# A two-layer transformer block on one core: gates in four PSUM tiles, a step's pacing, and where two norms stand

## The chip, the cores and the metric

The kernel runs on one core of a Trainium2 chip. The time is what one execution takes on the device, in microseconds (us). The kernel before took 2803.42 us (median of three runs, 2800.37 to 2804.48).

Engine names in the profile: PE is TensorE (matrix products), DVE is VectorE, ACT is ScalarE, POOL is GpSimd, SP is SyncE, which here only issues DMAs. SBUF is the on-chip memory, PSUM the small accumulator memory that PE writes.

## The reference

Two layers work on 1024 tokens `x` and 256 context tokens `ctx` of width 1024. Cut to what matters:

```python
for l in range(2):
    mod = silu(c) @ w_ada[l] + b_ada[l]            # shift, scale, gate per column; the same with c_ctx
    h   = rms_norm(x, norm_g[l]) * (1 + scale) + shift          # and hc from ctx
    a_glu, a_gate, nq, nk, nv, n_gate, wq, wk, wv, w_gate, merge = split(h @ w_in[l])
    o_na = neighbourhood_attention(nq, nk, nv, ...)
    o_wa = window_attention(wq, wk, wv, ...)
    y_a = (silu(layer_norm(conv(glu(a_glu)))) * silu(a_gate)) @ w_proj_a
    y_b = (o_na * silu(n_gate)) @ w_proj_b
    y_c = (o_wa * silu(w_gate)) @ w_proj_c
    y = sigmoid(g_a) * y_a + sigmoid(g_b) * y_b + sigmoid(g_c) * y_c      # g_* from merge
    x = x + gate * (y @ w_o)
    # layer 0 does the same for ctx; layer 1 gives x alone
```

All is float32. The kernel returns x after layer 1.

## The kernel before

Everything is held transposed: features on the 128 partitions, tokens along the row. The tokens form three groups (`GROUPS`): 0 and 1 of 512 image tokens, 2 of the 256 context tokens. Layer 0 works on all three; the gates, projections and the output of layer 1 work on groups 0 and 1 only.

A float32 product is made of three: each operand is split into a high part and a low part (`hh`/`hl`, `ogh`/`ogl`, two planes of a weight), and PE does high by high, low by high and high by low for each of 8 chunks of 128 features (`product`, L714), 24 matmuls into one PSUM tile. The projections of the branches have 4 chunks, 12 matmuls.

**Order.** PE runs in the order of the program (`sched` asks for a manual schedule of PE). The other engines get an order from a list scheduler when the program is built; each engine then runs its instructions strictly in that order, and an instruction that waits holds all behind it. SP's DMA issues stand in such a queue too.

**PSUM.** `mm_tile` gives one of two tiles in turn (pool `ps_mm`, 2 buffers). `s_tile` gives the tiles of two further pools, `ps_s` and `ps_t`, in turn. `ps_tr` is one more tile, used for small products: the sums `ss_ps` and the broadcast `sr_ps` of a norm, and `ada_sum`. A new product into a tile waits until the last reader of the old one is done.

**A layer.** First the attention, with the projections of units (q, k, v columns) and GLU in between; then the gates of the merge; then branch b, c and a: for each branch the gate blocks and the projection. A gate block (`gate_blocks`, c = 0 to 3, one product per group) is `gate`: product into `gt_ps`, tanh on ACT, and an elementwise step on DVE (L852) that reads PSUM; then `gated`: GpSimd multiplies by the branch's values `ov` (L862), ACT rounds to the high part `ogh` (L863), and GpSimd subtracts for the low part `ogl` (L864). `project` then does 8 blocks f of products with `ogh`/`ogl`, in four PSUM tiles (`s_tile` and `mm_tile` in turn, `pp_ps`), and combines each with the merge gate `mg_in` that SP loads: L963 on DVE for branch b, L965 on DVE and L967 on GpSimd for c.

**Side work.** The modulation of the next layer (`ada_blocks`) is done on DVE beside these products: blocks of four steps, each a DMA of a piece of `w_ada` (`w_ada_s`, two buffers) and 4 instructions (L205, L207). In layer 1 only one of the two columns is needed, and a step has 2 instructions; there are 4 such blocks, 16 steps. Two small PE products (`ada_sum`, L183) sum a finished block up; they stand in PE's order three steps later. `Pace` spreads the steps: each PE chunk adds credit (its time times a share), and a step is issued while there is credit; each step yields its cost. Beside gate b a convolution's normalisation (`conv_norm`, L824, L831) is paced in the same way and finished before project b.

**From layer 0 to layer 1.** The output of layer 0 is normalised for layer 1. Group 0's norm is done within the output pass. Then unit 0 of layer 1 is projected: ten tiles of 128 tokens (0 to 3 of group 0, 4 to 7 of group 1, 8 and 9 of group 2), 8 chunks each, into the two `mm_tile` buffers; `out` evicts a tile: ACT L352, L358, L370 and DVE L353, L371. The norm of a group (`Norm.steps`) is: sums on PE (L252), a chain of small DVE steps (L257, L106 to L111), a diagonal on GpSimd (L261), a broadcast on PE (L264) copied by ACT (L265), and then for each of 8 chunks k DVE L272, ACT L273 (`hh`) and DVE L274 (`hl`). Groups 1 and 2 go through these steps after unit 0's first two tiles have been issued (L1264 to L1273).

Of the kernel before, what the change touches and what calls it, by code (L numbers as in the profile page):

```python
# [13 lines left out]
ALU = mybir.AluOpType  # L14
# [26 lines left out]
KC = 8  # L41
# [9 lines left out]
def hybrid_block_kernel(  # L51
# [9 lines left out]
    nc = tc.nc  # L61

    def f32(ap):
        return ap.bitcast(F32)
# [107 lines left out]
    def ada_blocks(items, pool):  # L172


        late = []

        def sums():
            while late:
                l, lc, j0, ncol, av = late.pop(0)
                pt = ps_tr.tile([128, 512], F32, tag="tr", name="ada_sum")  # L180
                for j in range(2):
                    for c in range(ncol):
                        nc.tensor.matmul(  # L183
                            pt[:, 2 * j + c:2 * j + c + 1], lhsT=av[:, c, j * 128:(j + 1) * 128], rhs=ones[:, 0:1],
                            start=True, stop=True
                        )
                nc.vector.tensor_tensor(
                    mods[l][:, j0:j0 + 2, 0:ncol], pt[:, 0:4].rearrange("p (j c) -> p j c", c=2)[:, :, 0:ncol],
                    lc["b_ada"][:, j0:j0 + 2, None].to_broadcast([128, 2, ncol]), ALU.add,
                )  # L190

        for l, lc, j0 in items:
            src = w_ada[l].rearrange("(k p) n -> p k n", p=128)
            ncol = 1 if l == L - 1 and j0 >= 16 else 2
            acc = pool.tile([128, 512], F32, tag="acc0", bufs=2, name="ada_acc")
            av = acc.rearrange("p (c n) -> p c n", c=2)
            for k0 in range(0, KC, 2):
                w = pool.tile([128, 512], F32, tag="acc1", bufs=2, name="w_ada_s")
                wv = w.rearrange("p (k n) -> p k n", k=2)
                nc.sync.dma_start(out=wv, in_=src[:, k0:k0 + 2, j0 * 128:j0 * 128 + 256])  # L200
                for k in range(k0, k0 + 2):
                    for c in range(ncol):
                        s = sc_t[:, k, c:c + 1]
                        if k == 0:
                            nc.vector.tensor_scalar(av[:, c], wv[:, 0], s, None, ALU.mult)  # L205
                        else:
                            nc.vector.scalar_tensor_tensor(  # L207
                                av[:, c], wv[:, k - k0], s, av[:, c], ALU.mult, ALU.add
                            )
                yield 2 * ncol * 490.0  # L210
                if k0 == 4:
                    sums()
            late.append((l, lc, j0, ncol, av))
        yield 6000.0
        sums()
# [168 lines left out]
    def project_unit(l, u, h, pa, st, ws=None, unit=None, begin=0):  # L384

        if ws is None:
            ws = unit_weights(wU[l, u], pa)
            yield SWITCH_NS
        unit = unit or Unit(l, u, pa, st)
        for t in range(begin, 10):  # L390
            ps = mm_tile("u_ps")
            for k in range(KC):
                ns = unit.chunk(t, k, ws[k], h, ps)
                if k < KC - 1:
                    yield ns
            unit.out(t, ps)
            yield ns
        unit.close()
# [277 lines left out]
    def run(gen):  # L676
        for _ in gen:
            pass
# [30 lines left out]
    def product(w, kn, hx, n, ps):  # L709

        hh, hl = hx
        for k in range(kn):
            for i, (b, a) in enumerate(((0, hh), (0, hl), (1, hh))):
                nc.tensor.matmul(  # L714
                    ps[:, 0:n], lhsT=w(k, b), rhs=a[:, k, 0:n],
                    start=(k == 0 and i == 0), stop=(k == kn - 1 and i == 2),
                )
            if k < kn - 1:
                yield 3 * max(n / 2.4, 107)
# [4 lines left out]
    def mm_tile(name):  # L724
        return ps_mm.tile([128, 512], F32, tag="mm", name=name)

    flip = [0]

    def s_tile(name):
        flip[0] ^= 1  # L730
        if flip[0]:
            return ps_s.tile([128, 1024], F32, tag="s", name=name)
        return ps_t.tile([128, 1024], F32, tag="t", name=name)
# [112 lines left out]
    def gate(w, h, gi, t):  # L846

        n = GROUPS[gi][1]
        ps = mm_tile("gt_ps")
        yield from product(w, KC, h[gi], n, ps)  # L850
        nc.scalar.activation(t, ps[:, 0:n], AF.Tanh, scale=0.5)
        nc.vector.scalar_tensor_tensor(t, t, 1.0, ps[:, 0:n], ALU.add, ALU.mult)  # L852
        yield 3 * max(n / 2.4, 107)

    def gated(br, c, gi, t, ov, og):

        o, n = GROUPS[gi]
        a0, a1 = t, ov[:, 0:n]
        if br == "b" and gi < 2:
            a0 = a0.rearrange("p (r b c) -> p r b c", r=8, b=8)  # L860
            a1 = a1.rearrange("p (b r c) -> p r b c", b=8, r=8)
        nc.gpsimd.tensor_tensor(a0, a0, a1, ALU.mult)  # L862
        nc.scalar.activation(og[gi][0][:, c, :], t, AF.Copy)  # L863
        nc.gpsimd.tensor_tensor(og[gi][1][:, c, :], t, f32(og[gi][0][:, c, :]), ALU.subtract)  # L864

    def gated_tiles(po, ngr):
        og = []
        for gi in range(ngr):
            n = GROUPS[gi][1]
            og.append((  # L870
                po.tile([128, 4, n], F32R, tag=f"ogh{gi}", name=f"ogh{gi}"),
                po.tile([128, 4, n], F32R, tag=f"ogl{gi}", name=f"ogl{gi}"),
            ))
        return og
# [55 lines left out]
    def gate_blocks(l, br, h, pw, px, og, ngr, side):  # L930

        ws = [load_block(wF[l, I0[br]], pw)]
        for c in range(4):
            w = ws.pop(0)
            if c < 3:
                ws.append(load_block(wF[l, I0[br] + c + 1], pw))
            for gi in range(ngr):
                o, n = GROUPS[gi]
                ov = px.tile([128, 544], F32, tag="cv", bufs=1, name="ov")
                nc.sync.dma_start(out=ov[:, 0:n], in_=act_d[br][c][:, o:o + n])  # L940
                t = pw.tile([128, 512], F32, tag="t", bufs=3, name="gt_t")[:, 0:n]
                along(gate(w, h, gi, t), side)
                gated(br, c, gi, t, ov, og)
# [110 lines left out]
    def advance(gen, tiles):  # L1054
        for _ in range(KC * tiles):
            next(gen)
# [19 lines left out]
    with side_pool(0, "st", False) as st:  # L1076
# [15 lines left out]
        step = norm.steps(0, xs[0], g)  # L1092
# [61 lines left out]
        unit0 = project_unit(0, 0, h, pa, state, ws0, units[0], 4)  # L1154
# [4 lines left out]
        step = norm.steps(0, xs[2], g)  # L1159
# [5 lines left out]
    for l in range(L):  # L1165
# [15 lines left out]
        for nm in ORDER:  # L1181
            i = int(nm[1])
# [23 lines left out]
        with side_pool(l, "pc", True) as pools["pc"]:  # L1206
# [6 lines left out]
            og = gated_tiles(po, ngr)  # L1213
# [6 lines left out]
        if l + 1 < L:  # L1220
            cols += [(l + 1, lc_next, j) for j in range(0, 16, 2)]
        side = Pace(ada_blocks(cols, px), SHARE[1])
        for br in "bca":
            if br != "b":
                og = gated_tiles(po, ngr)
# [31 lines left out]
        def first_norm():  # L1257
            yield
            yield from norms[0].steps(l + 1, y[0], g)

        step = first_norm()
# [3 lines left out]
        unit0 = project_unit(l + 1, 0, h, pa, state, ws0)  # L1265
        steps = [norms[gi].steps(l + 1, y[gi], g) for gi in (1, 2)]
        advance(unit0, 1)
        next(steps[0])
        next(steps[1])
        advance(unit0, 1)  # L1270
        for step in steps:
            run(step)
        run(unit0)  # L1273
        sw.close()
# [88 lines left out]
```

## Time and profile before

| | |
|---|---|
| median of three runs | 2803.42 us |
| the profiled execution: its own time / span in the trace | 2803.28 / 2801.5 us |
| PE busy | 2701.9 us (96%) |
| VectorE / ScalarE / GpSimd busy | 1775.5 (63%) / 1132.6 (40%) / 897.1 us (32%) |
| mean granted TensorE clock | 0.989 |

PE counts as busy from a matmul's start to its end, and matmuls overlap, so it is at 96% even where it isn't at its best rate; the gaps between matmuls and the stretches at a lower granted clock show where time is left. A wait list gives, for each engine, what an instruction waited for last. Granted clock 1.00 is the upper level (2.4 GHz), 0.5 the lower (1.2 GHz); a value between is a mean over the stretch.

### The profile page before, as it was taken

Reading aid. Unit: us, or ns where it says so; the run is one execution under the profiler, and the core shown is the slowest. Engines: PE = TensorE matmul, PEld = TensorE weight load, DVE = VectorE, ACT = ScalarE, POOL = GpSimd, SP = SyncE. Lnnn points to the kernel's source line nnn. Section 1 sums busy time; section 2 is a strip of 40 time slices with the busy share of each in tenths; the row PEclk is TensorE's granted clock in tenths of the full one; section 3 lists DMA queues with packets and bytes.
Section 4 is the critical chain, followed back from the end, with each engine's and each line's share of the span. In section 5 each row is a group of like instructions: output and inputs, shape, how many; then the busy total and the mean of one; then the engine's idle time right before and its main releaser. Section 6 shows DMA issues by size and latency. Waiting matters only on the chain. (4 is left out here: it accounts for less than half of the span.)

```text
span 2801.5 us, 43631 instructions
## 1 busy us (share of the span) xinstructions
PE 2701.9 (96%) x14996; PEld 2354.5 (84%) x14996; DVE 1775.5 (63%) x3816; ACT 1132.6 (40%) x2500; POOL 897.1 (32%) x1148
## 2 busy tenths in 40 slices
PE   7899999999999999999999899999999999989999
PEld 3899999988888887888888899989888788767887
DVE  4667776766699905777365566666665798351162
ACT  2466666666411114121333356655555322322220
POOL 0034465633300004256501133465434100426610
PEclk9999999999999999999999999999999999989999
DMA  7355443211233322745364355452212333263343
GB/s 249 102 167 151 132 126 99 72 55 39 88 113 122 121 87 89 215 131 151 113 201 131 99 152 155 134 141 76 74 54 69 114 131 121 82 195 106 102 146 110
DMA packets 321293, 337.35 MB, mean 120 GB/s; under 512 B 81840, under 2 KB 240688, under 8 KB 321072
## 3 DMA queue, kind: packets, MB, share of 16 engines
q1 hardware_dynamic: 300848, 296.81, 35.8%
q10 hardware_dynamic: 17280, 28.32, 2.7%
q0 software_dynamic: 2944, 9.44, 0.8%
q8 instruction: 118, 1.93, 0.3%
q14 instruction: 103, 0.84, 0.1%
HBM read 244.02 MB, written 90.44 MB: 119 GB/s over the span
## 5 line engine op out<-in xcount | busy, mean ns | idle before, releaser
L714 PE MATMUL mg_ps<-hh,wf 128*128 128x512 f32 (+1 forms) x1920 | 563.3, 373 | 2.3 <-POOL wf L670 1.3
L339 PE MATMUL u_ps<-wu,hh 128*128 128x384 f32 (+2 forms) x1872 | 487.2, 343 | 18.2 <-ACT hh L273 12.3
L714 PEld LDWEIGHTS mg_ps<-hh,wf 128*128 128x128 f32 x1920 | 347.2, 188 | 71.5 <-POOL wf L670 2.1
L670 POOL TENSOR_TENSOR wf<-rf,wf 128x512 fp32r<-128x512 f32 x114 | 152.5, 1338 | 674.9 <-ACT wf L669 674.7
L714 PE MATMUL mg_ps<-hl,wf 128*128 128x512 f32 (+1 forms) x960 | 358.6, 374 | 0.0
L608 POOL TENSOR_SCALAR p<-p,rd 128x640 f32<-128x640 f32 (+1 forms) x288 | 216.4, 752 | 407.4 <-DVE rd L606 235.8
L339 PEld LDWEIGHTS u_ps<-wu,hh 128*128 128x128 f32 x1872 | 320.8, 192 | 23.9 <-ACT hh L273 12.8
L600 ACT ACTIVATE p<-p,nmx 128x641 f32<-128x641 f32 (+3 forms) x288 | 222.1, 771 | 237.2 <-DVE nmx L596 113.6
L339 PE MATMUL u_ps<-wu,hl 128*128 128x384 f32 (+2 forms) x936 | 313.6, 335 | 0.7 <-DVE hl L274 0.7
L714 PE MATMUL gt_ps<-hh,wf 128*128 128x512 f32 (+1 forms) x960 | 287.5, 380 | 8.2 <-DVE gt_t L852 5.4
L669 ACT ACTIVATE wf<-rf 128x512 fp32r<-128x512 f32 x240 | 150.6, 628 | 354.7 <-PE pp_ps L714 184.9
L714 PE MATMUL pp_ps<-ogh,wf 128*128 128x512 f32 (+1 forms) x960 | 282.2, 377 | 3.0 <-ACT ogh L863 2.6
L618 DVE TENSOR_TENSOR pt<-tp,pt 128x640 fp32r<-128x640 f32 (+1 forms) x288 | 215.8, 749 | 100.3 <-ACT pt L617 97.9
L714 PEld LDWEIGHTS gt_ps<-hh,wf 128*128 128x128 f32 x960 | 176.5, 190 | 46.5 <-DVE gt_t L852 6.9
L914 ACT ACTIVATE mg_t<-mg_ps 128x512 f32<-128x512 f32 (+1 forms) x120 | 66.7, 555 | 365.0 <-PE mg_ps L714 350.6
L714 PEld LDWEIGHTS pp_ps<-ogh,wf 128*128 128x128 f32 x960 | 177.9, 192 | 37.5 <-ACT ogh L863 3.1
L714 PEld LDWEIGHTS mg_ps<-hl,wf 128*128 128x128 f32 x960 | 180.5, 188 | 31.3
L614 PE MATMUL tp<-ident,p 128*128 128x128 f32 x1280 | 187.5, 273 | 17.8 <-DVE pt L618 9.8
L772 DVE SCALAR_TENSOR_TENSOR cv_out<-cv_in,lc_conv_w,cv_out 128x1024 f32<-128x1024 f32 (+1 forms) x192 | 194.5, 1013 | 0.0
L614 PEld LDWEIGHTS tp<-ident,p 128*128 128x128 f32 x1280 | 153.6, 141 | 45.4 <-POOL p L608 13.4
L617 ACT ACTIVATE pt<-tp 128x640 fp32r<-128x640 f32 (+1 forms) x288 | 181.8, 631 | 20.9 <-PE tp L614 19.6
L714 PE MATMUL pp_ps<-ogl,wf 128*128 128x512 f32 (+1 forms) x480 | 181.5, 378 | 3.6 <-POOL ogl L864 3.6
(172 smaller groups left out, 5498.1 us busy)
## 6 DMA issues: line engine op xcount, KB each, us to landing
rf<-in_wF SPq DMA_DIRECT2D x144, 256.0 KB, 2.8
ru<-in_wU SPq DMA_DIRECT2D x104, 192.0 KB, 3.6
bias<-in_na_bias SPq DMA_DIRECT2D x96, 192.0 KB, 2.6
w_ada_s<-in_w_ada SPq DMA_DIRECT2D x64, 256.0 KB, 3.2
nrm<-qk_d SPq DMA_DIRECT2D x40, 320.0 KB, 4.0
rf<-in_wP SPq DMA_DIRECT2D x48, 256.0 KB, 2.7
rf<-in_wO SPq DMA_DIRECT2D x48, 256.0 KB, 3.2
v_d<-vr SPq DMA_DIRECT2D x80, 128.0 KB, 2.1
```

The costliest lines, as they stand in the source:

```text
L339: nc.tensor.matmul(ps[:, c0:UW], lhsT=a[:, k, off * 128:(off + 1) * 128], rhs=w[:, b, c0:UW], start=(k == 0 and i == 0), stop=(k == KC - 1 ...
L600: nc.scalar.activation(self.p[:, 0:n], self.p[:, 0:n], AF.Exp, bias=m, scale=1.0 if sink is None else -1.0, accum_out=self.den)
L608: nc.gpsimd.tensor_scalar(p, p, rd, 1.0, ALU.mult, ALU.mult)
L614: nc.tensor.transpose(tp[:, c * 128:(c + 1) * 128], self.p[:, c * 128:(c + 1) * 128], ident)
L617: nc.scalar.activation(self.pt[:, 0:nch, 0, :], tv, AF.Copy)
L618: nc.vector.tensor_tensor(self.pt[:, 0:nch, 1, :], tv, f32(self.pt[:, 0:nch, 0, :]), ALU.subtract)
L669: nc.scalar.activation(w[:, 0, 0:n, :], raw[:, 0:n, :], AF.Copy)
L670: eng.tensor_tensor(w[:, 1, 0:n, :], raw[:, 0:n, :], f32(w[:, 0, 0:n, :]), ALU.subtract)
L714: nc.tensor.matmul(ps[:, 0:n], lhsT=w(k, b), rhs=a[:, k, 0:n], start=(k == 0 and i == 0), stop=(k == kn - 1 and i == 2),)
L772: nc.vector.scalar_tensor_tensor(r, a[:, k:k + n], tap, r, ALU.mult, ALU.add)
L914: nc.scalar.activation(t[:, 0:n], ps[:, 0:n], AF.Tanh, scale=0.5)
```

## The change

Four edits. `gate` takes its PSUM tile from `s_tile` and `mm_tile` in turn, so four tiles instead of two. In `gated`, the low part of the last block of a branch (c = 3) is computed on VectorE instead of GpSimd: 15 instructions, 9 in layer 0 and 6 in layer 1. A modulation step always costs 4 x 490 ns in the pacing; before it was 2 x 490 in layer 1's 16 steps, so only these change. And the norms of groups 1 and 2 are cut up: the sums of group 1 after tile 0, its broadcast and group 2's sums after tile 1, and then one step k after every second chunk of tiles 2 and 3 for group 1, and of tiles 4 and 5 for group 2.

```diff
@@ ada_blocks
-                yield 2 * ncol * 490.0
+                yield 4 * 490.0
                 if k0 == 4:
                     sums()
@@
-    flip = [0]
+    flip, turns = [0], [0]
@@ gate
-        ps = mm_tile("gt_ps")
+        turns[0] ^= 1
+        ps = s_tile("gt_ps") if turns[0] else mm_tile("gt_ps")
@@ gated
-        nc.gpsimd.tensor_tensor(og[gi][1][:, c, :], t, f32(og[gi][0][:, c, :]), ALU.subtract)
+        eng = nc.vector if c == 3 else nc.gpsimd
+        eng.tensor_tensor(og[gi][1][:, c, :], t, f32(og[gi][0][:, c, :]), ALU.subtract)
@@ end of layer 0
         advance(unit0, 1)
         next(steps[0])
+        advance(unit0, 1)
+        next(steps[0])
         next(steps[1])
-        advance(unit0, 1)
         for step in steps:
+            for i in range(2 * KC):
+                next(unit0)
+                if i % 2 == 0:
+                    next(step)
             run(step)
         run(unit0)
```

Line numbers behind L846 are one higher in the changed kernel and behind L863 two: `ogl` is L864 before and L866 after, the combination of branch b L963 and L965.

PE, after tile 1 of unit 0. `ss_ps` are the sums and `sr_ps` the broadcast of a norm; `hh_16251` and `hl_16252` belong to group 0. Before:

```order
L339 MATMUL u_ps<-wu,hl_16252 128x384
L264 MATMUL sr_ps<-diag,ones 128x512
L264 MATMUL sr_ps<-diag,ones 128x256
L339 MATMUL u_ps<-wu,hh_16251 128x384 x2
L339 MATMUL u_ps<-wu,hl_16252 128x384
```

Now, at the same place:

```order
L339 MATMUL u_ps<-wu,hl_16252 128x384
L264 MATMUL sr_ps<-diag,ones 128x512
L252 MATMUL ss_ps<-ones,sqa 128x1 x2
L339 MATMUL u_ps<-wu,hh_16251 128x384 x2
L339 MATMUL u_ps<-wu,hl_16252 128x384
```

Group 2's sums have come here from their place after tile 0, and its broadcast has gone behind the first chunk of tile 4, 17 chunks later.

DVE at the same stretch. `y_13090` is group 1's data and `y_13091` group 2's; L353 and L371 evict a tile of unit 0. Before, from the eviction of tile 1 to that of tile 2:

```order
L371 TENSOR_TENSOR vr<-u_ps,vr 128x2x64
L272 SCALAR_TENSOR_TENSOR y_13090<-y_13090,gcol_15726,sqa 128x512 x3
L274 SCALAR_TENSOR_TENSOR hl_16868<-y_13090,mod_128,hh_16867 128x512 x3
L272 SCALAR_TENSOR_TENSOR y_13090<-y_13090,gcol_15726,sqa 128x512 x3
L274 SCALAR_TENSOR_TENSOR hl_16868<-y_13090,mod_128,hh_16867 128x512 x3
L272 SCALAR_TENSOR_TENSOR y_13090<-y_13090,gcol_15726,sqa 128x512 x2
L272 SCALAR_TENSOR_TENSOR y_13091<-y_13091,gcol_15726,sqa 128x256
L274 SCALAR_TENSOR_TENSOR hl_16868<-y_13090,mod_128,hh_16867 128x512 x2
L274 SCALAR_TENSOR_TENSOR hl_16897<-y_13091,mod_128,hh_16896 128x256
L272 SCALAR_TENSOR_TENSOR y_13091<-y_13091,gcol_15726,sqa 128x256 x3
L274 SCALAR_TENSOR_TENSOR hl_16897<-y_13091,mod_128,hh_16896 128x256 x3
...
L353 TENSOR_REDUCE ss<-usq 128x4
```

Now, around the eviction of tile 2:

```order
L272 SCALAR_TENSOR_TENSOR y_13090<-y_13090,gcol_15726,sqa 128x512
L111 SCALAR_TENSOR_TENSOR n_rstd<-rs_a,n_rstd 128x2
L274 SCALAR_TENSOR_TENSOR hl_16872<-y_13090,mod_128,hh_16871 128x512
L109 SCALAR_TENSOR_TENSOR rs_a<-n_rstd,n_var 128x2
L353 TENSOR_REDUCE ss<-usq 128x4
L110 TENSOR_TENSOR rs_a<-rs_a,n_rstd 128x2
L274 SCALAR_TENSOR_TENSOR hl_16872<-y_13090,mod_128,hh_16871 128x512
L111 SCALAR_TENSOR_TENSOR n_rstd<-rs_a,n_rstd 128x2
L371 TENSOR_TENSOR vr<-u_ps,vr 128x2x64
L109 SCALAR_TENSOR_TENSOR rs_a<-n_rstd,n_var 128x2
L272 SCALAR_TENSOR_TENSOR y_13090<-y_13090,gcol_15726,sqa 128x512
```

Before, all 16 steps k of both groups but the last half step stand ahead of tile 2's eviction; now four of group 1's L272 and three of its L274 do, with group 2's small chain (128x2) between them.

DVE in layer 1, from the end of gate b into project b. `ogl_26750` is the low part of group 1's last block; L852 (now L853) belongs to the gate, L831 to the convolution's normalisation. Before:

```order
L852 SCALAR_TENSOR_TENSOR gt_t<-gt_t,gt_ps 128x512
L831 SCALAR_TENSOR_TENSOR ln_in<-ln_s,ln_in 128x512
L963 SCALAR_TENSOR_TENSOR y_27213<-mg_in,pp_ps 128x512
L963 SCALAR_TENSOR_TENSOR y_27214<-mg_in,pp_ps 128x512
L205 TENSOR_SCALAR ada_acc<-w_ada_s,sc_t 128x256
L207 SCALAR_TENSOR_TENSOR ada_acc<-w_ada_s,sc_t,ada_acc 128x256 x3
L963 SCALAR_TENSOR_TENSOR y_27213<-mg_in,pp_ps 128x512
L963 SCALAR_TENSOR_TENSOR y_27214<-mg_in,pp_ps 128x512
L207 SCALAR_TENSOR_TENSOR ada_acc<-w_ada_s,sc_t,ada_acc 128x256 x4
L187 TENSOR_TENSOR mod_128<-ada_sum,lc_b_ada_12430 128x2
```

Now:

```order
L853 SCALAR_TENSOR_TENSOR gt_t<-gt_t,gt_ps 128x512
L831 SCALAR_TENSOR_TENSOR ln_in<-ln_s,ln_in 128x512
L866 TENSOR_TENSOR ogl_26750<-gt_t,ogh_26749 128x512
L965 SCALAR_TENSOR_TENSOR y_27213<-mg_in,pp_ps 128x512
L965 SCALAR_TENSOR_TENSOR y_27214<-mg_in,pp_ps 128x512
L205 TENSOR_SCALAR ada_acc<-w_ada_s,sc_t 128x256
L207 SCALAR_TENSOR_TENSOR ada_acc<-w_ada_s,sc_t,ada_acc 128x256 x3
L965 SCALAR_TENSOR_TENSOR y_27213<-mg_in,pp_ps 128x512
L965 SCALAR_TENSOR_TENSOR y_27214<-mg_in,pp_ps 128x512
L207 SCALAR_TENSOR_TENSOR ada_acc<-w_ada_s,sc_t,ada_acc 128x256 x4
L965 SCALAR_TENSOR_TENSOR y_27213<-mg_in,pp_ps 128x512
L965 SCALAR_TENSOR_TENSOR y_27214<-mg_in,pp_ps 128x512
```

The low part has come to DVE, and the first block's sum (which L187 reads) stands later: its PE products follow 54 matmuls later in PE's order than before, and two of the four sums have moved from project b into gate c.

## Rows read from the trace of the kernel before

**Rows 1.** Windows: length, busy us per engine, PEclk (granted clock), DMA share, GB/s.

```profile
1240.00:1255.00 15.00, 13.02 (x59) 11.33 (x58) 11.43 (x16) 3.13 (x6) 8.51 (x7) 0.77 0.45 137
1305.00:1320.00 15.00, 12.25 (x58) 10.25 (x57) 8.30 (x14) 0.63 (x1) 9.44 (x8) 0.89 0.35 104
1565.00:1580.00 15.00, 9.03 (x37) 9.06 (x38) 7.56 (x21) 4.68 (x13) 0.00 (x0) 0.66 0.35 108
2472.00:2496.00 24.00, 18.19 (x70) 14.38 (x69) 12.68 (x23) 2.53 (x4) 5.37 (x4) 0.86 0.69 222
2496.00:2520.00 24.00, 20.53 (x79) 16.46 (x78) 13.41 (x23) 1.90 (x3) 4.17 (x3) 0.86 0.59 179
```

**Rows 2.** Waits of PE, 1540 to 1625: total us, times, longest.

```profile
PE u_ps L339 <- ACT hh L273: 8.3, 1, 8.3
```

**Rows 3.** Timeline of DVE, unit 0 and norms: start, us, instruction, [idle, releaser].

```profile
1549.97 0.16 DVE L110 TENSOR_TENSOR rs_a<-rs_a,n_rstd 128x2 f32<-128x2 f32 x1
...
1553.56 2.08 DVE L272 SCALAR_TENSOR_TENSOR y<-y,gcol,sqa 128x512 f32<-128x512 f32 x3 [0.33 <-ACT sqa L265]
...
1570.21 0.41 DVE L353 TENSOR_REDUCE ss<-usq 128x4 f32<-128x256 f32 x1
1570.54 0.28 DVE L371 TENSOR_TENSOR vr<-u_ps,vr 128x128 fp32r<-128x128 f32 x1
```

**Rows 4.** Timeline of PE, tile 4 of unit 0.

```profile
1570.97 0.98 PE L339 MATMUL u_ps<-wu,hh 128*128 128x384 f32 x2 [8.30 <-ACT hh L273]
...
1576.67 0.52 PE L339 MATMUL u_ps<-wu,hh 128*128 128x384 f32 x2
...
1577.20 0.52 PE L339 MATMUL u_ps<-wu,hh 128*128 128x384 f32 x2
```

**Rows 5.** Timeline of ACT, eviction of tile 4 of unit 0.

```profile
1577.93 0.39 ACT L352 ACTIVATE usq<-u_ps 128x256 f32<-128x256 f32 x1 [6.36 <-PE u_ps L339]
```

**Rows 6.** Waits of PE, layer 0, gate c to gate a.

```profile
PE gt_ps L714 <- DVE gt_t L852: 3.5, 3, 2.0
PE gt_ps L714 <- DVE mg_in L965: 2.7, 1, 2.7
```

**Rows 7.** Timeline of DVE, project c of layer 0, first and last blocks.

```profile
1256.88 0.68 DVE L965 SCALAR_TENSOR_TENSOR mg_in<-mg_in,pp_ps 128x512 f32<-128x512 f32 x1
...
1309.56 0.41 DVE L965 SCALAR_TENSOR_TENSOR mg_in<-mg_in,pp_ps 128x256 f32<-128x256 f32 x1
...
1312.95 1.60 DVE L965 SCALAR_TENSOR_TENSOR mg_in<-mg_in,pp_ps 128x512 f32<-128x512 f32 x3
```

**Rows 8.** Waits of PE, layer 0, gate b and project b.

```profile
PE gt_ps L714 <- DVE gt_t L852: 2.0, 1, 2.0
...
PE pp_ps L714 <- POOL ogl L864: 0.6, 1, 0.6
```

**Rows 9.** Waits of PE, layer 1, gate b and project b.

```profile
PE ada_sum L183 <- DVE ada_acc L207: 9.3, 3, 4.7
PE pp_ps L714 <- ACT ogh L863: 2.6, 1, 2.6
PE pp_ps L714 <- POOL ogl L864: 1.3, 2, 0.8
```

**Rows 10.** Timeline of DVE, layer 1, gate b into project b.

```profile
2458.72 5.04 DVE L831 SCALAR_TENSOR_TENSOR ln_in<-ln_s,ln_in 128x512 f32<-128x512 f32 x4 [0.67 <-ACT ln_s L830]
...
2473.13 1.31 DVE L205 TENSOR_SCALAR ada_acc<-w_ada_s,sc_t 128x256 f32<-128x256 f32 x1 [1.76 <-DMA w_ada_s<-in_w_ada]
...
2480.38 1.01 DVE L207 SCALAR_TENSOR_TENSOR ada_acc<-w_ada_s,sc_t,ada_acc 128x256 f32<-128x256 f32 x2 [1.48 <-DMA w_ada_s<-in_w_ada]
```

**Rows 11.** Waits of PE, layer 1, projects c and a.

```profile
PE pp_ps L714 <- POOL ogl L864: 1.7, 2, 0.8
```

**Rows 12.** Lines L207, L864: ns min/median/max, first and last start, forms.

```profile
L207 DVE SCALAR_TENSOR_TENSOR ada_acc<-w_ada_s,sc_t,ada_acc x196: 468/480/1599, 1135.3 to 2516.0; 128x256 f32<-128x256 f32 x196
...
L864 POOL TENSOR_TENSOR ogl<-gt_t,ogh x60: 722/1294/1734, 1067.6 to 2665.6; 128x512 fp32r<-128x512 f32 x48, 128x256 fp32r<-128x256 f32 x12
```

## The prediction, made before the result was known

> **What bounds the kernel now.** PE does: it is busy for 96% of the span, so I looked first for where it isn't at its rate, and took two views for that. The windows give each stretch's granted clock: it stands at 1.00 nearly everywhere, and falls in five short stretches [rows 1]. The wait lists of PE say what it waited for there. Each of these stretches lies beside one of the four edits. The first is unit 0 of layer 1 [rows 2 to 5], then gate c to gate a of layer 0 [rows 6, 7], gate b of layer 0 [rows 8], gate b and project b of layer 1 [rows 9, 10], and the start of projects c and a of layer 1 [rows 11]. A lost microsecond of PE in them is a microsecond of the span, since PE is the bound on both sides of each. All durations are from the profiled execution, 2803.28 us, which is 0.14 us from the median of 2803.42; the sum is made against 2803.28.
>
> **Unit 0 and the norms.** The list puts PE's 8.3 us down to ACT's `hh` [rows 2], and the reader should see that it was something else. PE starts tile 4 at 1570.97 [rows 4], and tile 4 uses the PSUM tile of tile 2. Tile 2's last reader is L371 on DVE, which ran 1570.54 to 1570.82, right behind L353 at 1570.21 [rows 3]: the order of before has all steps of both groups ahead of them. So the wait is for an eviction held up in DVE's queue. Behind the wait the clock is at the lower level: tile 4's eight chunks take from 1570.97 to ACT's eviction at 1577.93 [rows 4, 5], 6.96 us, where eight at the later pitch (1577.20 - 1576.67 = 0.53) take 4.2; 2.7 us are lost. The rest of the lowered 5.1 us of that window (15 x 0.34, [rows 1]) lies inside the wait.
>
> Now the evictions of tiles 2 and 3 stand among group 1's steps. I follow DVE's new order from the first L272. It started at 1553.56 [rows 3], and may now start earlier, since group 2's sums no longer stand ahead of group 1's chain; for the low end I leave it there. Up to tile 4's last operand come 15 steps at 2.08/3 = 0.69 [rows 3], 10.4; two evictions at 0.33 + 0.28, 1.2; and the 12 small instructions of group 2's chain at 0.16, 1.9: 1567.1. Then group 2's first step, of half the length (0.4 is an estimate from 0.69), and the last L274, 0.69: 1568.2. The last chunk ends 0.5 later, at 1568.7, against 1577.93: a gain of 9.2. The other end is that nothing waits at tile 4, and 8.3 + 2.7 = 11.0 is gained. I take 10.5, nearer to this end, since all of the assumed durations are those of single instructions, which overlap in part. PE's new wait is at group 2's sums: they need `ps_tr`, which ACT must first have copied for group 1; behind them is all of tile 2. The broadcast of group 2 waited for that same copy before, so I count nothing for it. If the clock falls there too, the end is 6. SP's loads of tables and biases move by a few places in its queue, all beside products that don't read them; if they came late, the attention would wait, which is the case "given back" below. POOL's diagonal for group 2 (two of six instructions) has tile 2 and 3 as its cover.
>
> **Gate c to gate a, layer 0.** PE waits 3.5 us in gate c for L852, the reader of one of two PSUM tiles, and 2.7 at gate a's first product for L965 [rows 6]; the clock costs 15 x 0.23 = 3.4 and 15 x 0.11 = 1.6 [rows 1]. Four tiles let PE run ahead in gate c. But project c already has four tiles, and there the view of DVE is the one to read: from its first L965 of f = 0 at 1256.88 to that of f = 7 at 1312.95 are 56.1 us, 8.0 per block [rows 7]. PE needs (12 + 12 + 6) x 0.236 = 7.1 (0.53/3 us for 384 columns gives 0.236 for 512). So this stretch runs at DVE's pace, with two modulation steps and more between its L965s. What PE gains in gate c (3.5 and up to 3.4) it waits for in project c. What stays is the end: with the turn of `s_tile`, gate a's first product takes a tile whose last reader is the L965 of f = 6, group 2, done at 1309.56 + 0.41 = 1309.97, and not that of f = 7, group 0, at 1312.95 + 0.68 = 1313.63 [rows 7]: 3.6 us, and the 1.6 of the clock. I take 5.2. Ends: 0, if DVE is later still by its three new instructions (3 x 0.69 = 2.1) and more; 11.2, if all of it returns.
>
> **Gate b, layer 0.** 2.0 us for L852 and 0.6 for `ogl` [rows 8]. Behind them project b waits for the same DVE and the side norm. I take 0.7, the low part on DVE; ends 0 and 2.6.
>
> **Gate b, layer 1.** 2.6 for `ogh` and 1.3 for `ogl` [rows 9]. Ahead of the last L852 on DVE stands 5.04 us of L831 [rows 10], which four PSUM tiles don't shorten: PE arrives earlier and waits longer. Only the low part's 1294 ns on GpSimd [rows 12] against 0.69 for a DVE step is shorter, about 0.6 for each of two groups. I take 1.3; ends 0 and 3.9.
>
> **The sums in project b, layer 1.** PE waits 9.3 us in three waits for L207 [rows 9]: a block's sums stand where the block isn't done yet. The first block takes from 2473.13 to 2481.39 on DVE, 8.3 us, with waits for DMA between its steps [rows 10]. Before, a step costs 980 ns against a credit of 0.6 of PE's time, 1.6 us of PE for a step and 6.5 for a block: less than the 8.3 that it takes. Now it is 3.3 for a step, 13.1 for a block: more than 8.3. And the first sums stand 54 matmuls, 12.7 us, later, past the 4.7 us that they lacked. So the waits go. The clock's loss in the two windows is 24 x 0.14 = 3.4 each [rows 1]; each fall comes after one of these waits. I take three quarters, 5.0. Sum 14.3; ends 5, if only the first and longest wait goes, and 16.0. Two of the sums now stand in gate c, where DVE has little to do; they cost PE the same.
>
> **Projects c and a, layer 1.** Two waits of 0.8 for `ogl`, 1.7 in all [rows 11]. DVE does it in 0.69 instead of 1.29, and one of two tiles is early anyway: 1.2; ends 0 and 1.7.
>
> Here a rule speaks against the edit. A DVE instruction with two SBUF inputs does get longer beside GpSimd in this trace: L207 takes 468 ns at its shortest, 480 in the median and 1599 at its longest [rows 12], and L831 needs 5.04 for four [rows 10]. The Trainium skill, "SBUF — State Buffer", section "Who interferes with whom", says that such an instruction and a GpSimd one that reads SBUF exclude each other on a shared port for the whole instruction, and the second waits. L207's longest agrees with it, 1.1 us above its shortest. By that rule the new low parts, with both inputs in SBUF, would gain nothing where GpSimd is at work beside them; the sum would be lower by about 3. It is rival two.
>
> **The sum.** 10.5 + 5.2 + 0.7 + 1.3 + 14.3 + 1.2 = 33.2; 2803.28 - 33.2 = 2770.1, so 2770. The ends sum to 11 and 46.4 (2792 and 2757), but won't all fall to one side: its own range is 2764 to 2776.
>
> **Rivals.**
> 1. All that the lists show returns, gate c's waits too: the 8.0 a block in project c is then not DVE's own work, but waits for GpSimd or a DMA that come earlier when PE does. Then 6.0 more there, 1.9 in layer 0's gate b, 2.6 in layer 1's: 43.7 in all, 2760. For it: the 8.0 is a distance of starts, and doesn't tell work from waits. Against it: PE had spare PSUM tiles in project c before and still waited.
> 2. The low parts on DVE are held by GpSimd's instructions, and delay L965 and L852 behind them. The terms 0.7, 1.3 and 1.2 go, and the end of project c is 3 us later, so that of its 5.2 only 2 stay: 33.2 - 3.2 - 3.2 = 26.8, so 2776. Against it: GpSimd loses the same 15 instructions.
> 3. Given back: unit 0 ends 11 us earlier, but what follows (unit 1's weights, the attention's tables) comes at its old time, and a wait takes the place. Then 10.5 goes, and half of the 5.0 of the clock in the sums' term: 33.2 - 13.0 = 20.2, so 2783. For it: these loads stand in SP's one queue. Against it: they are issued behind unit 0's own stores, which come earlier as well.
> 4. Slower: PE, run at DVE's pace all through project c of layer 0, with a wait in each block, is given the lower clock there. At 1.2 GHz a block takes 14.2 instead of 8.0, eight blocks 50 us more, and the 5.2 is gone: 2770 + 50 + 5 = 2825. It decides from where five of the eight blocks are at the lower level, 31 against the other terms' 28. For it: each of the five falls [rows 1] stands beside a wait. Against it: what they cost is 1.6 to 5.1 us each, and PE ran through the rest at 1.00.
> 5. The edits don't do what they say: the sums wait still, for the DMA, and DVE's evictions still come late. Then only some 5 us: 2798.
>
> **How the numbers follow.** Forecast 0.55, rival 1 0.11, rival 2 0.16, rival 3 0.10, rival 4 0.03, rival 5 0.05. 2757 to 2785 holds rivals 1 to 3 and the forecast's ends, leaving out the far cases and parts of the others, under 0.2. What a measurement of this kernel can tell from no change is about 0.2%, 5.6 us. Faster by more holds in all but rival 4 and part of rival 5: 0.93; within 0.2%: 0.03; slower: 0.04.
>
> **What would show it.** In the changed profile, the wait of 8.3 before tile 4 is gone, and the window behind it has clock 1.00; the list has no `ada_sum` wait over 0.5 us in layer 1; PE waits for L967 or its neighbours inside project c, about 1 us a block, and gate a starts without a wait; L866 on DVE takes 0.7 to 1.8. A wait of several us between unit 0 and unit 1 would make rival 3 right, a granted clock near 0.5 over project c rival 4, and `ada_sum` waits of the old size would break the largest term.

## The result and the profile after

The changed kernel took 2772.18 us (median of four runs, 2769.40 to 2772.55), the kernel before on the same chips 2803.95. The ratio is 0.9886 with a 95% interval of 0.9869 to 0.9903: 31.8 us faster. The prediction was 2770, in a range of 2757 to 2785. The profiled execution has a span of 2770.5, 31.0 less than before.

Both traces can be compared by stage. I take the start of the first product of each stage on PE and subtract: what the changed kernel is ahead at the end of a stage minus what it was ahead at its start is what the stage gave (0.4 to 0.5 come before gate b, where nothing was changed). The changed kernel was profiled three times in all (the two others beside experiments below).

| stage | predicted | first profile | second | third |
|---|---|---|---|---|
| gate b and project b, layer 0 | 0.7 | -0.2 | 0.9 | 1.0 |
| gate c, project c, gate a, layer 0 | 5.2 | 6.3 | 7.1 | 6.9 |
| unit 0 and the norms | 10.5 | 9.9 | 9.9 | 9.9 |
| the rest of the attention, merge gates | 0 | -3.2 | -0.5 | 0.1 |
| gate b and project b, layer 1 | 1.3 + 14.3 | 17.4 | 17.7 | 16.7 |
| gate c to the end, layer 1 | 1.2 | 0.3 | 0.4 | 0.3 |

The windows of the changed kernel that answer to [rows 1], with the same columns. They are shifted with the work, and one for the start of project b in layer 1 is added (2446 to 2458):

```profile
1240.00:1255.00 15.00, 12.48 (x71) 9.72 (x70) 10.68 (x21) 3.48 (x7) 6.26 (x5) 1.00 0.47 145
1305.00:1320.00 15.00, 15.00 (x76) 12.30 (x75) 8.85 (x15) 1.86 (x3) 10.83 (x9) 1.00 0.36 101
1548.00:1563.00 15.00, 13.69 (x79) 13.31 (x78) 13.57 (x34) 8.45 (x19) 2.57 (x4) 1.00 0.11 36
2446.00:2458.00 12.00, 8.69 (x30) 6.45 (x29) 8.59 (x10) 3.92 (x7) 2.98 (x2) 0.86 0.75 257
2458.00:2482.00 24.00, 24.00 (x107) 19.56 (x107) 17.38 (x29) 3.38 (x6) 6.47 (x5) 1.00 0.80 261
2482.00:2506.00 24.00, 24.00 (x110) 19.68 (x109) 12.35 (x22) 3.65 (x6) 8.14 (x7) 1.00 0.57 185
```

All five stretches of before have their full clock back. From 2458 on PE is busy throughout project b of layer 1, where it was busy for 18.2 and 20.5 of 24 us. What is left is the start of that project, 0.86. The wait lists of PE say what stands there now: first around unit 0 (1530 to 1600), against [rows 2]:

```profile
PE sr_ps L264 <- POOL diag L261: 1.3, 1, 1.3
PE u_ps L339 <- ACT wu L292: 0.9, 2, 0.5
PE ss_ps L252 <- ACT sqa L265: 0.7, 1, 0.7
PE u_ps L339 <- DVE wu L293: 0.6, 1, 0.6
```

Then layer 0 from gate c's end to gate a (1240 to 1320), against [rows 6]:

```profile
PE pp_ps L714 <- ACT ogh L864: 1.5, 3, 0.7
PE pp_ps L714 <- DVE ogl L866: 1.0, 3, 0.6
PE pp_ps L714 <- DVE mg_in L967: 0.2, 1, 0.2
```

Then gate b and project b of layer 1 (2430 to 2520), against [rows 9], where no `ada_sum` waits any more:

```profile
PE pp_ps L714 <- ACT ogh L864: 3.1, 1, 3.1
PE ln_pr L822 <- DVE ln_in L824: 0.4, 1, 0.4
PE pp_ps L714 <- DVE ogl L866: 0.2, 1, 0.2
```

And projects c and a of layer 1 (2520 to 2720), against [rows 11]:

```profile
PE pp_ps L714 <- DVE ogl L866: 0.5, 2, 0.2
```

### The profile page after: what moved, and what is told of

Its sections match the earlier page's. It is cut to its first block, busy times and chain, and to the rows that moved or that the text cites. A ratio compares the mean times of both kernels' runs of the same rounds, so it can differ in the third digit from the quotient of the medians.

```text
span 2770.5 us, 43625 instructions
## 1 busy us (share of the span) xinstructions
PE 2692.1 (97%) x14996; PEld 2343.4 (85%) x14996; DVE 1783.6 (64%) x3831; ACT 1134.5 (41%) x2500; POOL 882.6 (32%) x1133
## 5 line engine op out<-in xcount | busy, mean ns | idle before, releaser
L714 PE MATMUL wo_ps<-hh,wf 128*128 128x512 f32 (+1 forms) x640 | 184.8, 373 | 0.0
```

The source lines that it names most:

```text
L714: nc.tensor.matmul(ps[:, 0:n], lhsT=w(k, b), rhs=a[:, k, 0:n], start=(k == 0 and i == 0), stop=(k == kn - 1 and i == 2),)
```

## The experiments

Runs of the kernel before vary by more than 5 us between executions, so each kernel was timed beside the kernel before on the same chip, and ratios are to that. Differences in us are worked out from the ratio and 2802.

### Each edit alone

The four edits of the diff were put into the kernel before, one at a time. The cut shows the main lines of each; e4 also moves the sums and the broadcasts, as in the diff of the change.

```diff
 e1: +        turns[0] ^= 1
     +        ps = s_tile("gt_ps") if turns[0] else mm_tile("gt_ps")
 e2: +        eng = nc.vector if c == 3 else nc.gpsimd
 e3: +                yield 4 * 490.0
 e4: +            for i in range(2 * KC):
     +                next(unit0)
     +                if i % 2 == 0:
     +                    next(step)
```

Expected of the gates in four tiles: 

> The kernel before with only the first edit: gate products in four PSUM tiles in turn. Theory (from the trace of the changed kernel, where gate c of layer 0 is 7 us shorter, project c 2 us longer and gate a 1.4 us shorter): 5 to 7 us faster than before. Rival 1: the low parts still come from GpSimd, so project c waits longer for them, and what gate c gains is given back: 0 to 2 us faster. Rival 2: everything the wait lists show around gates comes back, 11 us or more.

Expected of the low part on VectorE: 

> The kernel before with only the second edit: the low part of the last gate block on VectorE. Theory: 0.6 us at each of the places where PE waited for a GpSimd low part, 2 to 3 us faster, with DVE's L864 at 0.69 us where GpSimd is idle and up to 1.6 us where it works. Rival (the port rule): DVE's low part is held by GpSimd's work, nothing gained: within 1 us of before.

Expected of the pacing: 

> The kernel before with only the third edit: layer 1's modulation steps paced at half the rate. Theory: the three waits at ada_sum (9.3 us) and both falls of the clock behind them go: 13 to 16 us faster. Rival: only the first and longest wait goes, 5 us; or the waits move into gate c, 0 to 5 us.

Expected of the norms: 

> The kernel before with only the fourth edit: norms of groups 1 and 2 between unit 0's products. Unit 0 ends 9.9 us earlier. Theory A (what follows is held by transfers that come at a later time of their own): the attention gives 3 us back, as in the changed kernel, so 6 to 7 us faster. Theory B (the attention's 3 us has to do with the other edits or with chance): 9 to 10 us faster.

| edit alone | ratio, 95% interval | us |
|---|---|---|
| e1, four tiles | 0.9975 (0.9965 to 0.9985) | -7.0 |
| e2, low part on VectorE | 0.9990 (0.9982 to 0.9998) | -2.8 |
| e3, pacing | 0.9959 (0.9947 to 0.9971) | -11.5 |
| e4, norms | 0.9967 (0.9955 to 0.9979) | -9.2 |
| sum | | -30.5 |
| all four (the changed kernel beside e5) | 0.9886 (0.9872 to 0.9900) | -31.9 |

The sum is the whole within its error, which for the four together is some 6 us. The stages say it more sharply: gate c to gate a gives 6.4 in e1 alone, gate b and project b of layer 1 17.1 in e3 and unit 0 9.9 in e4, all as with the four together. So the edits don't feed on each other at these places. e1 is at the upper end of its theory, and neither of its rivals. e2 gains what its theory said; no gain at all lies just outside its interval, so by the time the port rule's case is unlikely and not excluded. By the stages e2 has 0.6 in each of projects c and a of layer 1, as the changed kernel has, and no gain in layer 0. e4's 9.2 lies where theory B put it, but its interval, 5.9 to 12.6, holds theory A as well. By the stages unit 0's own gain is 9.9 in this profile too, and the attention gave back 2.1 here, 3.2, 0.5 and -0.1 in the three profiles of the changed kernel. And e1 to e3, which leave unit 0 as it was, are 0.6, 1.3 and 2.4 slower than the profile of before in the same stage. So kernels differ there by nearly as much without the edit: the one profile of before seems to have been quick in that stage, and the 3.2 can't be put down to the edits.

e3 falls short of 13 us. Its trace shows no `ada_sum` wait, so the step is right; what is off is the size. The wait lists of the three kernels that keep the old pacing (e1, e2 and e4, in that order, 2430 to 2520) have less of it than the one profile of before, which has 9.3 [rows 9]:

```profile
PE ada_sum L183 <- DVE ada_acc L207: 6.0, 3, 2.8
```

```profile
PE ada_sum L183 <- DVE ada_acc L207: 7.4, 3, 3.4
```

```profile
PE ada_sum L183 <- DVE ada_acc L207: 6.5, 3, 3.0
```

In these three, gate b and project b of layer 1 are 3.1 to 4.1 us shorter than in the profile of before, without the edit. That execution, though its time was the median, seems to have had a dear stage there. Against a usual one the edit is worth some 13.5 (17.1 in e3's trace, less 3.6), or 12.6 with the 0.9 that gate c loses to the two sums that moved into it, and e3's interval of 8.1 to 14.9 us holds that.

### What held tile 4 of unit 0

The prediction took the wait of 8.3 us as one for tile 2's eviction, against the profile, which names ACT's `hh`. This kernel gives unit 0 four PSUM tiles and leaves the norms where they were.

```diff
-            ps = mm_tile("u_ps")
+            ps = s_tile("u_ps") if l > 0 and u == 0 and t % 2 else mm_tile("u_ps")
```

Expected: 

> The kernel before, with unit 0 of layer 1 in four PSUM tiles instead of two and no other change; the norms stay where they were, and so does DVE's order. Theory (tile 4 waits for the eviction of tile 2, which is queued on DVE behind the norms' steps): tile 4 starts at once, the wait of 8.3 us and the lower clock behind it go, 9 to 11 us earlier at the end of unit 0. Rival (the releaser that the profile names, ACT's hh, is the real one): the wait stays at 8 us, no gain.

Its ratio is 0.9960 (0.9945 to 0.9974), 11.2 us faster. PE's list around unit 0 (1540 to 1590) has no such wait, its longest are these, and DVE's timeline has tile 2's eviction at the old time:

```profile
PE u_ps L339 <- ACT wu L292: 0.8, 1, 0.8
PE sr_ps L264 <- ACT sqa L265: 0.8, 1, 0.8
```

```profile
1570.23 0.41 DVE L353 TENSOR_REDUCE ss<-usq 128x4 f32<-128x256 f32 x1
1570.56 0.28 DVE L371 TENSOR_TENSOR vr<-u_ps,vr 128x128 fp32r<-128x128 f32 x1
```

L353 and L371 run within 0.02 us of where they ran before [rows 3], `hh` is made by the same instructions in the same order, and PE doesn't wait. So the wait was for the tile, and the name in the list was wrong. By the stage unit 0 gains 11.0 in this kernel, and 9.9 in the changed one. Behind it the attention of this profile gave 3.1 back, and gate b and project b of layer 1, which this edit doesn't touch, were 3.3 shorter, as in e1, e2 and e4; so the 11.2 agrees with the 11.0 in sum and not stage by stage.

### DVE's load at gate c

The prediction said that project c of layer 0 runs at DVE's pace. This kernel is the changed one with fewer modulation steps there:

```diff
-                yield 4 * 490.0
+                yield 4 * (640.0 if l == 0 else 490.0)
```

Expected: 

> The changed kernel with layer 0's modulation steps paced at 490/640 of their rate, so that DVE has less to do in gate c and project c. Theory (project c starts late because DVE, 92% busy there, brings gate c's last outputs late): the 4 us of waits for ogh and ogl at the start of project c shrink to 2 or less, 2 to 3 us faster than the changed kernel. Rival (these waits are the plain length of the chain from the last product over ACT, DVE and GpSimd to ogh): no difference, or slower where the modulation's end moves towards the end of the layer.

The changed kernel ran again beside it: 

> The changed kernel once more, beside the others on this chip, as their base: 30 to 33 us faster than before.

The ratios are 0.9886 (0.9870 to 0.9901) and 0.9886 (0.9872 to 0.9900): no difference, to within some 4 us. Yet the waits that the theory named did shrink. Its 4 us were those of e1 (2.6 and 1.3); the changed kernel has 1.5 and 1.0, and 1.2 and 0.8 in the profile beside this one. PE's list from 1238 to 1320:

```profile
PE pp_ps L714 <- DVE mg_in L967: 0.8, 2, 0.5
PE gt_ps L714 <- DVE mg_in L967: 0.4, 1, 0.4
PE pp_ps L714 <- ACT ogh L864: 0.4, 1, 0.4
```

The waits at the start are down to 0.4, but PE now waits for L967 further on. With the modulation sums taken off at 0.9 us each, the first block f of project c is 2.3 us shorter than in the profile beside it, as the theory said, and the fourth to sixth are 1.3 longer together: by the stage 1.1 us is left. The other differences are sums that moved: 1.2 us came in project b and 0.9 in gate c, and 2.1 was lost in gate a and project a, where two more of PE's sums stand. The theory of the waits holds, but half of its price goes back in the same project.

### Three further edits, and what they did

The trace of the changed kernel suggests three: the broadcast `sr_ps` of group 2 a little later, since PE now waits 1.3 us there for the diagonal; a faster side norm in layer 1, whose last steps on DVE stand ahead of the 3.1 us wait for `ogh`; and the lighter pacing.

```diff
-        for step in steps:
+        for s, step in enumerate(steps):
             for i in range(2 * KC):
                 next(unit0)
-                if i % 2 == 0:
+                if i % 2 == 0 and i >= 4 * s:
                     next(step)
...
-            norming = Pace(side_norm(), SHARE[0])
+            norming = Pace(side_norm(), SHARE[0] if l == 0 else 1.0)   # e8; 0.88 in e9 and e12; unchanged in e10
...
-                yield 4 * 490.0
+                yield 4 * (560.0 if l == 0 else 490.0)                 # e9 and e10 alone
```

The first two together, with a share of 1.0: 

> The changed kernel with two more edits that its trace suggests: the broadcast and steps of group 2's norm start four chunks later, and layer 1's side norm is paced at a share of 1.0 instead of 0.8. Theory: PE's 1.3 us wait for the diagonal at tile 4 goes, and the 3.2 us wait for ogh before project b of layer 1, with the lower clock behind it, gets shorter: 3 to 6 us faster than the changed kernel. Rival: the side norm's PE products then wait for DVE in gate b, and nothing is gained.

All three, with 0.88: 

> The changed kernel with three small edits: group 2's broadcast four chunks later (1.1 us at unit 0 in the run with both edits), layer 0's modulation steps at 490/560 of their rate (the waits before project c of layer 0 were 2 us shorter at 490/640), and layer 1's side norm at a share of 0.88 (at 0.8 PE waits 3.1 us for ogh behind it, at 1.0 it waits 3.1 us for the norm's sums ahead of it). Theory: 2 to 4 us faster than the changed kernel, with the side norm's wait split in two and smaller in sum. Rival: the share only moves the wait, and the rest is 1 us or less.

The first and the last: 

> The same without the share: group 2's broadcast four chunks later and layer 0's modulation steps at 490/560 of their rate. Theory: 1 to 2 us faster than the changed kernel. Rival: no difference.

The changed kernel beside the last two: 

> The changed kernel once more, as the base of these two: 30 to 33 us faster than before.

| kernel | ratio, 95% interval | median us, and of the changed kernel beside it |
|---|---|---|
| e8, later broadcast, share 1.0 | 0.9877 (0.9864 to 0.9891) | 2767.40, 2769.20 |
| e9, later broadcast, share 0.88, pace 560 | 0.9885 (0.9870 to 0.9900) | 2770.63, 2770.05 |
| e10, later broadcast, pace 560 | 0.9900 (0.9884 to 0.9917) | 2774.75, 2770.05 |

Expected were 3 to 6, 2 to 4 and 1 to 2 us less than the changed kernel; by the medians e8 takes 1.8 less, e9 0.6 more and e10 4.7 more. None is clearly better than the changed kernel, and by the stages each for a reason of its own. The later broadcast gives 1.1 to 1.2 us in unit 0 in all three. The share of 1.0 moves the side norm's wait: PE's list from 2340 to 2510 has 3.1 us again, ahead of the gates.

```profile
PE ln_ps L801 <- DVE ln_s L798: 3.1, 1, 3.1
```

With 0.88 that is gone, and the wait for `ogh` is 1.2 us; gate b and project b of layer 1 are 5 to 6 us shorter than in the changed kernel, though the merge gates ahead of them, where the norm now takes more of DVE, are longer by about 2. The pace of 560 is what costs. PE's list of e10 around the start of project c in layer 0 (1240 to 1270), and DVE's timeline there:

```profile
PE pp_ps L714 <- ACT ogh L864: 5.3, 2, 3.2
PE pp_ps L714 <- DVE ogl L866: 2.5, 2, 2.2
```

```profile
1249.41 0.68 DVE L853 SCALAR_TENSOR_TENSOR gt_t<-gt_t,gt_ps 128x512 f32<-128x512 f32 x1
1250.00 4.70 DVE L207 SCALAR_TENSOR_TENSOR ada_acc<-w_ada_s,sc_t,ada_acc 128x256 f32<-128x256 f32 x4
1254.63 0.68 DVE L866 TENSOR_TENSOR ogl<-gt_t,ogh 128x512 fp32r<-128x512 f32 x1
1255.23 0.41 DVE L853 SCALAR_TENSOR_TENSOR gt_t<-gt_t,gt_ps 128x256 f32<-128x256 f32 x1
```

Four modulation instructions, 4.70 us in all where four at their median take 1.9 [rows 12], have come between the last gate steps, and the low part that project c waits for stands behind them. The granted clock fell there as well. The window after it, from 1255 to 1270:

```profile
1255.00:1270.00 15.00, 14.64 (x61) 12.77 (x61) 8.30 (x18) 1.31 (x3) 6.83 (x6) 0.67 0.62 196
```

So less load at a worse place costs more than more load at a better one; with 640 the steps fell better. The last run keeps the broadcast and the share of 0.88 and leaves the pacing alone.

Expected: 

> The changed kernel with layer 1's side norm at a share of 0.88 and group 2's broadcast four chunks later; layer 0's pacing is left as it is. Theory: the two gains seen by stage in the run with three edits stay (about 5 us from gate b to project b of layer 1, 1.1 us in unit 0), and its loss of some 7 us at the start of project c of layer 0 goes, since it came with layer 0's pacing: 36 to 40 us faster than before, some 6 below the changed kernel. Rival: the clock falls elsewhere, and the kernel is within 2 us of the changed one.

It took 2764.18 us, ratio 0.9866 (0.9849 to 0.9882), 36.4 us faster than before on its chip, the low end of what was expected; the changed kernel was 31.5 to 32.5 faster in its runs. By the stages, unit 0 gives 10.8, and all from there to gate c of layer 1 gives 18.3, against 9.9 and 14.2 to 17.3. Each of the two gains is seen at its place, but smaller than expected: 0.9 us, and 1.0 to 4.1. The intervals of the ratios overlap from 0.987 to 0.988, and the changed kernel didn't run on this chip; that this one is better by some 4 us is likely.

## Why the prediction was right

The largest terms, unit 0 and the sums, came for the reasons given. That the total was hit to some 2 us is luck in part: in the first profile the stages miss their terms by 0.6 to 3.2 us, some up and some down.

**Unit 0.** The step held as it was put: the releaser was misnamed, the eviction was the wait, and e5 shows it. In the changed kernel DVE's timeline has tile 2's eviction between group 1's steps:

```profile
1551.85 0.42 DVE L353 TENSOR_REDUCE ss<-usq 128x4 f32<-128x256 f32 x1
...
1553.19 0.29 DVE L371 TENSOR_TENSOR vr<-u_ps,vr 128x128 fp32r<-128x128 f32 x1
```

and tile 4 on PE starts without a wait and is stopped only behind its first chunk:

```profile
1555.33 0.51 PE L339 MATMUL u_ps<-wu,hh 128*128 128x384 f32 x2
...
1557.33 0.70 PE L264 MATMUL sr_ps<-diag,ones 128*128 128x256 f32 x2 [1.31 <-POOL diag L261]
...
1561.51 0.51 PE L339 MATMUL u_ps<-wu,hh 128*128 128x384 f32 x2
```

Counted at nothing was the diagonal of group 2, with "tile 2 and 3 as its cover". It isn't covered: the small chain ahead of it is spread among DVE's long steps, and PE waits 1.3 us. 11.0 less 1.3 is near the 9.9 measured; the low end of 9.2, which summed durations, was nearer than I thought.

**Gate c to gate a, layer 0.** The total was about right and the reason was not. The 8.0 us a block are DVE's own pace: from the L967 of f = 0 to that of f = 7 it is 56.2 us in the changed kernel, 56.1 before. The step that failed is "What PE gains in gate c (3.5 and up to 3.4) it waits for in project c". It took PE as tied to that pace. It set 7.1 a block for PE and left out PE's modulation sums, which stand among project c's products, and it didn't ask how far four tiles let PE run ahead of DVE. A window of before over the whole of project c shows PE busy for 60.25 of 63 us, and what is left is the 2.7 us before gate a [rows 6]:

```profile
1250.80:1313.80 63.00, 60.25 (x323) 51.40 (x321) 58.01 (x89) 6.72 (x12) 40.26 (x34) 0.99 0.61 183
```

60.25/8 is 7.5 a block. So PE went at its own pace, and DVE, at 92% busy, fell behind it by some 0.6 us a block. These rows are PE of before at the last matmul of group 0's product for f = 0 and for f = 7 (the second matmul of each row begins the next product):

```profile
1254.03 0.63 PE L714 MATMUL pp_ps<-ogh,wf 128*128 128x512 f32 x2
...
1305.63 0.63 PE L714 MATMUL pp_ps<-ogh,wf 128*128 128x512 f32 x2
```

The same of the changed kernel, and DVE's L967 of these two products:

```profile
1247.31 0.63 PE L714 MATMUL pp_ps<-ogh,wf 128*128 128x512 f32 x2
...
1302.97 0.93 PE L714 MATMUL pp_ps<-ogh,wf 128*128 128x512 f32 x2
```

```profile
1255.26 0.67 DVE L967 SCALAR_TENSOR_TENSOR mg_in<-mg_in,pp_ps 128x512 f32<-128x512 f32 x1
...
1311.49 1.27 DVE L967 SCALAR_TENSOR_TENSOR mg_in<-mg_in,pp_ps 128x512 f32<-128x512 f32 x2
```

Before, DVE was 2.9 us behind at f = 0 and 7.3 at f = 7 [rows 7]; now it is 8.0 and 8.5 behind. What PE gained in gate c became lead over DVE, and PE waits for it only late in the project, where a product finds its tile not yet read:

```profile
1296.09 0.50 PE L714 MATMUL pp_ps<-ogh,wf 128*128 128x512 f32 x1 [0.18 <-DVE mg_in L967]
```

Gate c gave 6.8 in all three profiles. Project c took back 1.1 to 1.9: its first block is 2.6 to 3.5 longer, where DVE brings the last gate blocks late (1.5 + 1.0 us in the list), its sixth and seventh 0.3 to 0.4 each, and its last, with the 2.7 us gone, 2.1 to 2.4 shorter. Gate a gave 1.4. The prediction had 3.6 and 1.6 for these last two; the 3.6 was the distance of two releases, where PE itself waited 2.7. Of the 11.2 of rival 1 that leaves 6.3 to 7.1, but not by its reason, since the 8.0 didn't shrink. The sign that was named for my step, about 1 us of waiting in each block, isn't in the trace, and neither is rival 4's lower clock, which hung on it.

**Gate b, layer 0.** As said, project b waits in place of the gate: the gate gave 2.2 us in each profile and project b took back 1.3 to 2.4, so 0.7 was within what the three show.

**Gate b and project b of layer 1.** For the gate, the tail of the side norm on DVE did stay, as said: 2.6 and 1.3 us of waits [rows 9] became 3.1 and 0.2, so 0.6 was gained and not 1.3: the waits for low parts fell by 1.1, and the one for `ogh` grew by 0.5, since DVE's new instruction for group 0 stands ahead of group 1's last gate step (e2, with this edit alone, has 3.1 as well). For the sums all three waits and both falls of the clock went; I had kept a quarter of the clock's 6.7. Two sums moved with their own 0.9 us into gate c, which the last two rows of the stage table show as a gain here and a loss there. What e1, e2 and e4 add is that the 9.3 itself was high for this kernel, by 2 to 3 us.

**The low parts.** Projects c and a of layer 1 gave 0.6 each, 1.2 as predicted. On the port rule the trace is on both sides. Line L866's durations (ns min/median/max) in the changed kernel, on GpSimd and on DVE:

```profile
L866 POOL TENSOR_TENSOR ogl<-gt_t,ogh x45: 735/1296/1576, 1067.1 to 2624.0; 128x512 fp32r<-128x512 f32 x36, 128x256 fp32r<-128x256 f32 x9
L866 DVE TENSOR_TENSOR ogl<-gt_t,ogh x15: 410/693/1562, 1122.0 to 2635.1; 128x512 fp32r<-128x512 f32 x12, 128x256 fp32r<-128x256 f32 x3
```

The median is 693 ns, and the longest, 1562, ran beside a GpSimd weight step in gate b of layer 1, longer than the 1294 it replaced:

```profile
2444.23 1.75 POOL L670 TENSOR_TENSOR wf<-rf,wf 128x512 fp32r<-128x512 f32 x1
```

```profile
2444.96 1.56 DVE L866 TENSOR_TENSOR ogl<-gt_t,ogh 128x512 fp32r<-128x512 f32 x1
```

That agrees with the Trainium skill, "SBUF — State Buffer", section "Who interferes with whom". Five of the 15 began inside such a step of GpSimd and took 1028 to 1562 ns; the other ten took 410 to 425 (256 columns) and 691 to 693. So in most places GpSimd wasn't at work at that moment, and projects c and a of layer 1 gain the full 0.6 each. Rival 2 falls.

**Given back.** Rival 3 said that what follows unit 0 might come at its old time. The first profile gave 3.2 us back in the attention, where one wait for DVE was 2.0 instead of 0.8 and the clock fell once. The others gave back 0.5 and nothing, and e1 to e3, without the edit, were up to 2.4 slower there than the profile of before. So rival 3 falls, and no run shows a cost of the change there.

## What to carry to other kernels

A wait for several things is named by the last that the profile knows; look at who still reads the buffer that the waiting instruction writes, and at what is queued ahead of that reader. Before PE is called bound by a slower engine behind it, count all that PE does in the stage and how far its buffers let it run ahead: with four tiles PE was up to 8.5 us ahead of DVE, and project c was over when that was just used up. And where an engine runs its queue in order, the place of side work can decide more than its amount, as with the pace of 560 here, so a pacing number is tried, and its effect read at the stage, not in the total.

## What the runs showed of the hardware that was not expected

The granted clock doesn't fall each time that the same waits come. In the attention the same stretch of work (within a microsecond), PE equally busy and with the same three waits of 2.3 us in all, was at 0.91 in the changed kernel (2160 to 2180) and at 1.00 in the one before (2174 to 2194):

```profile
2160.00:2180.00 20.00, 17.67 (x96) 14.97 (x95) 7.07 (x16) 8.34 (x17) 4.98 (x6) 0.91 0.22 66
```

```profile
2174.00:2194.00 20.00, 17.69 (x103) 15.01 (x102) 7.91 (x20) 9.11 (x19) 5.72 (x7) 1.00 0.21 62
```

What it cost is some 1.8 us (20 x 0.09, an estimate), as much as several of the terms above. What decides it is left open.
